# The last six down tiles and the second layer norm in four column chunks, with centred weights and a row sum gathered by DMA

## The chip, the cores and the metric

The kernel runs on one core of a Trainium2 chip. A core has five engines with queues of their own, which work in order: PE (matmuls), DVE (vector), ACT (scalar), POOL (GpSimd) and SP, which here only issues DMAs. POOL issues DMAs too, those that add to their destination among them. The metric is the device time of one execution in microseconds (us), the median of several. The profile is of one execution; it tells times on the chip, a line of the kernel and the names of the tiles for each instruction.

## The reference

One decoder layer runs over 1024 prompt rows and 8 sample rows: three branches with their gates, a layer norm, SwiGLU, a second layer norm. Only the end matters here:

```python
h = layer_norm(ALPHA * x + merged @ w_out, ln1_g, ln1_b)
gt, up = jnp.split(h @ w_gate_up, 2, axis=-1)
h = layer_norm(ALPHA * h + (jax.nn.silu(gt) * up) @ w_down, ln2_g, ln2_b)

def layer_norm(x, g, b):
    xf = x.astype(jnp.float32)
    mu = xf.mean(-1, keepdims=True)
    var = jnp.square(xf - mu).mean(-1, keepdims=True)
    y = (xf - mu) * lax.rsqrt(var + LN_EPS) * g.astype(jnp.float32) + b.astype(jnp.float32)
    return y.astype(x.dtype)
```

The model width is 1024 and the inner width 2816, so `w_down` has 22 blocks of 128 rows. Everything is in 32-bit floats.

## The kernel before

The data lie transposed: the 1024 features of a row are 8 tiles m of 128 partitions, and the 1032 rows (1024 + 8) are columns. A product in full precision is three matmuls, since each operand is split into a rounded high part and the rest: high by high, high by low, low by high (`mm3`, L115). `split` (L77) makes the high part on ACT (L79) and the low part on DVE (L80). Residuals are scaled, so that a product is added with the factor `SHARE`.

`gate_up_down` (L1244) runs the gate and up products and then the first 16 of the 22 blocks of the down product in units, by a scheme with fewer matmuls (7 products in place of 8, `fast_step`). A down unit j ends with two output tiles, zaf and zbf, of the rows m = 2j and 2j + 1; `FinishDown.done` (L1471) has POOL add them by DMA to h, which lies in the chip's memory as `scr_h`. The 16 blocks are done in two rounds of four units each. The last zaf and zbf are those of rows m = 6 and 7.

The last six blocks (`LAST`, blocks 16 to 21) are plain `mm3` products, made in `last_products` (L1344). Their moving operand is g (loaded and split by `last_rows`), their weights are the tiles wl0 to wl7, one for each m, with a raw load in two parts of 512 and 256 columns by SP (`half_raw`, L95, six raw buffers), and a split. `last_weights` is called for the first four from the end of `gate_up_down`, for the others from the first chunk's loop. The 1032 columns are taken in three chunks `CH` of 384, 390 and 258. For each chunk and each m there are 18 matmuls (6 blocks by 3) into a PSUM bank, and one DVE instruction adds the result to a tile acc of the row m, which SP loaded from `scr_h` as a whole (L1342, 516 KB).

The second norm of the chunks 0 and 1 is `layer_norm` (L957), a generator: column sums on DVE, a mean by matmuls with a matrix of ones, subtraction and squares, a variance in the same way, reciprocal root, scaling, affine on ACT, store by SP. It is stepped in the course of the next chunk (at the m in `NORM_AT`). The last chunk has its own, `last_layer_norm` (L992): matmuls with the matrix `shift` (L1019, L1020, L1029, L1030) take a part of the mean out early, sums run on DVE (L1010) and POOL (L1012), and after the last product four full-precision matmuls `le` (L1036 to L1039) give the mean and the mean of squares. Then come the subtraction of the mean in eight tiles on DVE and POOL (L1046), the reciprocal (L1047), eight multiplications (L1050), eight affines on ACT (L1362) and eight stores (L1363).

The order on each engine is decided by a scheduler when the program is built; it follows the order of the code, moved by when inputs are expected. `issue_after` and `behind` tie single instructions to others.

## Time and profile before

| | us |
|---|---|
| median of 3 runs | 1936.51 (1936.05 to 1939.27) |
| the profiled execution | 1938.83 |
| its span in the trace | 1937.1 |
| first product of the last six blocks | 1845.30 |
| last matmul of that stage starts | 1916.32 |
| PE busy | 1901.0 (98%) |
| DVE, ACT, POOL busy | 1389.0, 1001.8, 117.0 |

The page gives busy times, the chain that ended last (each step followed back to what released it), groups of instructions by line, and DMA issues with the time from issue to landing. A row of a timeline has the start, the length, the engine, the line, the operation, output and inputs, and in square brackets how long the engine stood idle before it and what ended that. Where two engines share the words SPq or POOLq, it is the queue of a DMA-issuing engine. Busy shares are means over the whole span: PE's 98% says little on the last 90 us, for which the prediction shows rows.

### The profile page before, as it was taken

The numbers are of one execution on the slowest core, as the hardware profiler recorded it, in microseconds if no ns is written. First come the engines' busy times: TensorE is split into PE (matmuls) and PEld (weight loads), VectorE is DVE, ScalarE is ACT, GpSimd is POOL, SyncE is SP. The second block draws the span as 40 slices with busy tenths as digits, with TensorE's granted clock in tenths as the row PEclk, the third lists the DMA queues.
The fourth block names the chain that finished last, engine by engine and source line by source line (L and its number), as shares of the span: only waits on it lengthen the run. The fifth ranks groups of instructions, "written<-read, shape, count | busy, mean of one in ns | idle before, by whom it ended". The sixth has DMA issues, their size and how long they took to land.

```text
span 1937.1 us, 37999 instructions
## 1 busy us (share of the span) xinstructions
PE 1901.0 (98%) x14716; PEld 1869.5 (97%) x14716; DVE 1389.0 (72%) x2738; ACT 1001.8 (52%) x2115; POOL 117.0 (6%) x168
## 2 busy tenths in 40 slices
PE   9999999999999999999999999999999999999996
PEld 8999999999999998888899999999999999999996
DVE  7878887877866655378887557775667667858467
ACT  6555565555655644388775234543433434636424
POOL 1000001110000000022110000000000000001001
PEclk9999999999999999999999999999999999999998
DMA  8545555446423376667534351123245345768542
GB/s 308 179 146 173 168 182 167 140 150 210 169 83 137 117 240 222 196 173 208 152 98 152 110 197 58 60 99 99 93 154 195 96 134 182 254 161 233 137 143 88
DMA packets 171637, 303.20 MB, mean 157 GB/s; under 512 B 19568, under 2 KB 86208, under 8 KB 171456
## 3 DMA queue, kind: packets, MB, share of 16 engines
q1 hardware_dynamic: 168384, 290.22, 45.8%
q0 software_dynamic: 3072, 10.55, 2.7%
q8 instruction: 115, 1.88, 0.4%
q14 instruction: 66, 0.54, 0.1%
HBM read 214.79 MB, written 90.09 MB: 157 GB/s over the span
## 4 chain that ended last, share of the span: by engine, by line
PE 84%; ACT 5%; DMA 4%; DVE 4%; issue 1%; SPq 0%; ACTq 0%; DVEq 0%
PE ub L250 5%; PE ub L248 5%; PE ub L249 5%; PE ubfg L248 4%; PE ubfg L249 4%; PE ubfg L250 4%; PE ud L250 3%; PE ud L249 3%; PE ud L248 3%; PE udfg L248 2%; PE udfg L249 2%; PE udfg L250 2%; PE op L120 2%; PE op L122 2%; PE op L121 2%; PE brs L120 2%
## 5 line engine op out<-in xcount | busy, mean ns | idle before, releaser
L605 ACT ACTIVATE bp<-bp,bst 128x257 f32<-128x257 f32 (+1 forms) x128 | 62.8, 493 | 17.7 <-DVE bst L601 17.3
L248 PE MATMUL ub<-th,u_4h 128*128 128x258 f32 x240 | 67.8, 283 | 1.3 <-ACT u2s L274 1.3
L248 PE MATMUL ub<-th,u_0h 128*128 128x258 f32 x240 | 68.0, 284 | 0.7 <-ACT zb L1490 0.6
L250 PE MATMUL ub<-th,u_4l 128*128 128x258 f32 x240 | 68.2, 284 | 0.0
L250 PE MATMUL ub<-th,u_0l 128*128 128x258 f32 x240 | 68.2, 284 | 0.0
L250 PE MATMUL ub<-th,u_2l 128*128 128x258 f32 x240 | 68.2, 284 | 0.0
L250 PE MATMUL uc<-th,u_3l 128*128 128x258 f32 x240 | 68.2, 284 | 0.0
L250 PE MATMUL ud<-th,u_1l 128*128 128x258 f32 x240 | 68.1, 284 | 0.0
L250 PE MATMUL ud<-th,u_5l 128*128 128x258 f32 x240 | 68.1, 284 | 0.0
L250 PE MATMUL ub<-th,u_6l 128*128 128x258 f32 x240 | 68.1, 284 | 0.0
L248 PE MATMUL ub<-th,u_6h 128*128 128x258 f32 x240 | 67.9, 283 | 0.0
L248 PE MATMUL uc<-th,u_3h 128*128 128x258 f32 x240 | 67.9, 283 | 0.0
L248 PE MATMUL ub<-th,u_2h 128*128 128x258 f32 x240 | 67.8, 283 | 0.0
L248 PE MATMUL ud<-th,u_5h 128*128 128x258 f32 x240 | 67.8, 282 | 0.0
L248 PE MATMUL ud<-th,u_1h 128*128 128x258 f32 x240 | 67.7, 282 | 0.0
L249 PE MATMUL ub<-tl,u_6h 128*128 128x258 f32 x240 | 67.7, 282 | 0.0
L249 PE MATMUL ud<-tl,u_5h 128*128 128x258 f32 x240 | 67.7, 282 | 0.0
L249 PE MATMUL uc<-tl,u_3h 128*128 128x258 f32 x240 | 67.6, 282 | 0.0
L249 PE MATMUL ub<-tl,u_4h 128*128 128x258 f32 x240 | 67.6, 282 | 0.0
L249 PE MATMUL ud<-tl,u_1h 128*128 128x258 f32 x240 | 67.6, 282 | 0.0
L249 PE MATMUL ub<-tl,u_0h 128*128 128x258 f32 x240 | 67.6, 282 | 0.0
L249 PE MATMUL ub<-tl,u_2h 128*128 128x258 f32 x240 | 67.6, 282 | 0.0
(954 smaller groups left out, 8228.3 us busy)
## 6 DMA issues: line engine op xcount, KB each, us to landing
ur<-win SPq DMA_DIRECT2D x120, 256.0 KB, 2.9
urfg<-wgu SPq DMA_DIRECT2D x80, 256.0 KB, 2.6
scr_f<-G SPq DMA_DIRECT2D x22, 516.0 KB, 3.2
f<-scr_f SPq DMA_DIRECT2D x16, 516.0 KB, 5.7
fs<-scr_t SPq DMA_DIRECT2D x16, 516.0 KB, 8.3
dck<-cmk SPq DMA_DIRECT2D x32, 256.0 KB, 3.7
dcv<-cmvT SPq DMA_DIRECT2D x32, 256.0 KB, 2.8
st<-scr_q SPq DMA_DIRECT2D x32, 256.0 KB, 5.1
```

The source lines that it names most:

```text
L120: nc.tensor.matmul(ps, sh, mh, start=opens and i == 0, stop=False)
L121: nc.tensor.matmul(ps, sh, ml, start=False, stop=False)
L122: self.last_mm = nc.tensor.matmul(ps, sl, mh, start=False, stop=closes and i == last).ins
L248: mm(sh[:, w], xh, start=opens and k == 0, stop=False)
L249: mm(sh[:, w], xl, start=False, stop=False)
L250: self.last_mm = mm(sl[:, w], xh, start=False, stop=k == 3).ins
L605: nc.scalar.activation(x, x, AF.Exp, bias=st[:, g:g + 1], scale=-1.0, accum_out=st[:, 4 + g:5 + g])
```

## The change

The last six blocks and the second norm are done in four chunks q of 258 columns (`QN`). What it rests on: if from each column of `w_down`'s last six blocks' contribution the mean over the 1024 features is taken out of the weights themselves, then the product adds nothing to a row's mean, and the mean is that of h alone, known before the products.

- `weight_means`, stepped in the units of `gate_up_down`, loads the weights of the last six blocks once more (SP, eight loads), sums them on DVE and gives `wbar`, minus the mean for each of the six blocks. `last_weights` adds it, on POOL, to the raw weights before they are split (two instructions for each m, of 512 and 256 columns).
- `row_sums` has POOL gather the sum over m of the rows of h by eight DMAs, the first plain, the others added to the same tile `rsum` in SBUF. It runs in the second round's units 1, 2 and 3. The last zaf and zbf, that are not in h yet when rows 6 and 7 are gathered, are added on DVE (`sums`), which then splits the sum.
- `residual` loads h in blocks r(q, kh) of four rows m and 258 columns (kh = 0: rows 0 to 3, by SP; kh = 1: rows 4 to 7, by POOL, for q = 0 in two halves). `centre` takes the mean from a block, with a mean made by two matmuls on `rsum`.
- `down_norm` does the chunks 0 to 2 (squares, folding, variance, reciprocal root, scaling, affine, a store for each block). The last chunk only squares, adds and has two `le` matmuls; its affines are shared by ACT and DVE.
- The matrix `shift`, `layer_norm` and `last_layer_norm` go.

The core of the diff:

```diff
@@ -1277,6 +1186,10 @@
             self.fast_step(st[u], i, moving[u[0]], finish[u])
             if i == 6:
                 del st[u]
+            if i in (2, 5):
+                next(means, None)
+            if u[0] == FAST - 1 and u[1] and i == 1:
+                self.row_sums(((6, 0, 1), (7, 2, 3), (4, 5))[u[1] - 1])
...
-                        4: lambda: self.last_rows(7, 4), 5: lambda: self.last_weights(0, 0),
-                        6: lambda: self.last_acc(0), 7: lambda: self.last_weights(1, 2),
-                        8: lambda: self.last_acc(1)}.get(n - len(todo) + 10)
+                        4: lambda: self.last_rows(7, 4), 5: self.last_weights,
+                        7: lambda: (self.last_weights(), self.residual(0, 0)),
+                        8: lambda: (self.last_weights(), self.residual(1, 0)), 9: self.last_weights}.get(
+                            n - len(todo) + 10)
...
+    def row_sums(self, rows):
+        for m in rows:
+            if m == 6:
+                self.rsum = self.zt("rsum")
+                self.nc.gpsimd.dma_start(self.rsum, self.scr["h"][:, m, :])
+            else:
+                self.nc.gpsimd.dma_start(self.rsum, self.scr["h"][:, m, :], accum_op=ALU.add)
...
+    def weight_means(self):
+        nc, (f0, nf) = self.nc, LAST
+        part = self.sm.tile([P, KT, nf], F32, tag="wpart", name="wpart", bufs=1)
+        for m in range(KT):
+            raw = self.zt(f"wsum{m}")[:, :nf * P]
+            nc.sync.dma_start(raw, self.io["wdn"][m][:, f0 * P:(f0 + nf) * P])
+            yield
+            nc.vector.tensor_reduce(part[:, m, :], raw.rearrange("p (k n) -> p k n", k=nf), axis=AX.X, op=ALU.add)
+            yield
+        self.wbar = self.sm.tile([P, nf], F32, tag="wbar", name="wbar", bufs=1)
+        nc.vector.tensor_reduce(self.wbar, part.rearrange("p m k -> p k m"), axis=AX.X, op=ALU.add)
+        nc.vector.tensor_scalar_mul(self.wbar, self.wbar, -1.0 / D)
...
+    def last_weights(self):
+        nc, m, (f0, nf) = self.nc, len(self.wl), LAST
+        if m % 2 == 0:
+            self.wslots = self.slot_pairs(m // 2, f"wl{m}")
+        hi, lo = (t.rearrange("p k n -> p (k n)") for t in self.wslots[m % 2])
+        for a, b in ((0, 4), (4, nf)):
+            n, w = (b - a) * P, slice(a * P, b * P)
+            raw = self.half_raw(self.io["wdn"][m][:, (f0 + a) * P:(f0 + b) * P], n, f"wl{m}r{a}")[:, :n]
+            blocks = raw.rearrange("p (k n) -> p k n", k=b - a)
+            nc.gpsimd.tensor_add(blocks, blocks, self.wbar[:, a:b].unsqueeze(2).to_broadcast([P, b - a, P]))
+            self.split(hi[:, w], lo[:, w], raw)
+        self.wl.append([(hi[:, k * P:(k + 1) * P], lo[:, k * P:(k + 1) * P]) for k in range(nf)])
...
+    def residual(self, q, kh):
+        t = self.zt(f"r{q}{kh}").rearrange("p (k n) -> p k n", k=4)
+        src = self.scr["h"][:, 4 * kh:4 * kh + 4, q * QN:(q + 1) * QN]
+        if kh == 0:
+            self.nc.sync.dma_start(t, src)
+        elif q == 0:
+            self.nc.gpsimd.dma_start(t[:, 0:2, :], src[:, 0:2, :])
+            self.nc.gpsimd.dma_start(t[:, 2:4, :], src[:, 2:4, :])
+        else:
+            self.nc.gpsimd.dma_start(t, src)
+        self.A[q, kh] = t
...
+    def sums(self):
+        nc = self.nc
+        mean, spare = self.slot_pairs(4, "rsum")
+        hi, lo = (t.rearrange("p k n -> p (k n)") for t in mean)
+        self.spare = [t.bitcast(F32) for t in spare]
+        for z in self.tail:
+            nc.vector.tensor_add(self.rsum, self.rsum, z)
+        self.split(hi, lo, self.rsum)
+        self.mean = hi, lo
...
+    def centre(self, q):
+        nc = self.nc
+        mu = self.bank("o", f"n2mu{q}")[:, :QN]
+        for n, t in enumerate(self.mean):
+            nc.tensor.matmul(mu, self.ones, t[:, q * QN:(q + 1) * QN], start=n == 0, stop=n == 1)
+        for kh in range(2):
+            nc.vector.tensor_sub(self.A[q, kh], self.A[q, kh], self.spread(mu))
...
+    def down_norm(self, q):
+        nc, r, vec = self.nc, self.A, self.vec
+        yield
+        if q < 2:
+            self.centre(q)
+        sq = self.spare
+        for kh in range(2):
+            nc.scalar.activation(sq[kh], r[q, kh], AF.Square)
+        nc.vector.tensor_add(sq[0], sq[0], sq[1])
+        s = self.fold(sq[0])
+        yield
+        var = self.col_mean(s, QN, f"n2va{q}")
+        rs = self.ph.tile([P, QN], F32, tag="rs", name=f"n2rs{q}", bufs=1)
+        nc.scalar.activation(rs, var, AF.Sqrt, bias=vec[:, V_EPS:V_EPS + 1])
+        nc.vector.reciprocal(rs, rs)
+        for kh in range(2):
+            nc.vector.tensor_mul(r[q, kh], r[q, kh], self.spread(rs))
+            for k in range(4):
+                self.affine(q, kh, k)
+            self.store(q, kh, 0, 4)
...
+        side, s2, sq = [self.down_norm(q) for q in range(3)], row("s2"), None
+        for n in side:
+            next(n)
+        self.sums()
+        for q, kh in ((2, 0), (3, 0), (0, 1), (1, 1), (2, 1), (3, 1)):
+            self.residual(q, kh)
+        go = {(1, 0): (0,), (1, 4): (0,), (2, 0): (1,), (2, 4): (1,), (3, 0): (2,), (3, 3): (2,)}
+        for q in range(4):
             for m in range(KT):
-                ps = product(m)
-                r = rs[m]
-                if m in NORM_AT:
-                    self.norm_step()
+                if len(self.wl) < KT:
+                    self.last_weights()
+                ps = self.bank(("mm", "s")[m % 2], f"dl{m}_{q}")[:, :QN]
+                cols = slice(q * QN, (q + 1) * QN)
+                self.mm3(ps, [(self.wl[m][k], tuple(a[:, cols] for a in self.g[k])) for k in range(nf)])
+                with self.tc.issue_after(self.last_mm):
+                    for n in go.get((q, m), ()):
+                        next(side[n], None)
+                    if (q, m) in ((1, 2), (2, 2)):
+                        self.centre(q + 1)
+                r = self.A[q, m // 4][:, m % 4, :]
                 nc.vector.scalar_tensor_tensor(r, ps, SHARE, r, op0=ALU.mult, op1=ALU.add)
-                if m == 1:
-                    nc.vector.tensor_add(s1, rs[0], r)
-                elif m > 1:
-                    nc.vector.tensor_add(s1, s1, r)
-            self.norm_start(self.layer_norm(c, rs, s1, V_G2, emit, "n2", c == 1))
+                if q == 3:
+                    sq = s2 if m == 0 else ph.tile([P, QN], F32, tag="sq", name=f"lsq{m}", bufs=2)
+                    nc.scalar.activation(sq, r, AF.Square)
+                    if 0 < m < 7:
+                        nc.vector.tensor_add(s2, s2, sq)
+        ones = self.ones.bitcast(F32)
+        e = self.bank("t", "le")[:, :QN]
+        nc.tensor.matmul(e, ones, s2, start=True, stop=False)
+        nc.tensor.matmul(e, ones, sq, start=False, stop=True)
+        rs = row("lrs")
+        nc.scalar.activation(rs, e, AF.Sqrt, bias=self.vec[:, V_EPS:V_EPS + 1])
+        nc.vector.reciprocal(rs, rs)
+        for kh in range(2):
+            nc.vector.tensor_mul(self.A[3, kh], self.A[3, kh], self.spread(rs))
+        for k in range(4):
+            self.affine(3, 0, k)
+            self.store(3, 0, k, k + 1)
+        for k in (3, 2, 1):
+            self.affine(3, 1, k, nc.vector)
+            self.store(3, 1, k, k + 1)
+        self.affine(3, 1, 0)
+        self.store(3, 1, 0, 1, nc.scalar)
```

The first place is POOL, around the last accumulates of zaf and zbf (line L1473 before, L1489 after). Names carry buffer numbers; what stands in brackets are the semaphores that an instruction waits for: DMASW for landings of POOL's DMAs, DMAHW for those of SP's, numbered in turn. Before, POOL's queue at this place is

```order
L1473 DMA scr_h<-zaf_23483 128x1032 [waits DMASW4_49,DVE_49]
L1473 DMA scr_h<-zbf_23516 128x1032 [waits DMASW5_49,Activation_49]
L1473 DMA scr_h<-zaf_23767 128x1032 [waits DMASW6_49,DVE_49]
L1473 DMA scr_h<-zbf_23798 128x1032 [waits DMASW7_49,Activation_49]
L1012 TENSOR_TENSOR ls_24366<-ls_24366,lsq_24510 128x258 [waits DMAHW0_49,DMAHW1_49,PE_49,Activation_49]
```

and now (L1267 is the addition of wbar, L1278 and L1279 are the halves of r(0, 1), L1281 the other r loads of POOL)

```order
L1489 DMA scr_h<-zaf_23796 128x1032 [waits DVE_49]
L1278 DMA r_23961<-scr_h 128x2x258
L1489 DMA scr_h<-zbf_23825 128x1032 [waits Activation_49]
L1267 TENSOR_TENSOR wl4r_23974<-wl4r_23974,wbar 128x512 [waits DMAHW0_49,Pool_49]
L1267 TENSOR_TENSOR wl4r_23979<-wl4r_23979,wbar 128x256 [waits DMAHW1_49,Pool_49]
L1267 TENSOR_TENSOR wl5r_24004<-wl5r_24004,wbar 128x512 [waits DMAHW2_49,Pool_49]
L1279 DMA r_23961<-scr_h 128x2x258 [waits DMASW6_49,DMASW0_49]
L1281 DMA r_23964<-scr_h 128x4x258
L1281 DMA r_23966<-scr_h 128x4x258
L1281 DMA r_23968<-scr_h 128x4x258 [waits DVE_49]
L1267 TENSOR_TENSOR wl5r_24009<-wl5r_24009,wbar 128x256 [waits DMAHW3_49,Pool_49]
L1267 TENSOR_TENSOR wl6r_24038<-wl6r_24038,wbar 128x512 [waits DMAHW4_49,Pool_49]
```

Behind these stand the other additions for wl6 and wl7. The load at L1279 waits for DMASW6 and DMASW0, the landings of the zaf and of the zbf above it; the loads and additions behind it are new on this queue, and the sums `ls` of the last chunk are gone from it.

The second place is PE's end. Before, behind the last products:

```order
L122 MATMUL dl_2_24602<-g7h_23701,wl3l_24062 128x258
L1019 MATMUL dl_2_24602<-c0h_24367,shift 128x258
L1020 MATMUL dl_2_24602<-c0l_24368,shift 128x258
L1036 MATMUL le_24371<-ls_24365,ones 128x258 [waits DVE_49]
L1037 MATMUL le_24372<-ls_24366,ones 128x258 [waits Pool_49]
L1038 MATMUL le_24371<-acc_24102,ones 128x258 [waits DMAHW3_49]
L1039 MATMUL le_24372<-lsq_24624,ones 128x258 [waits Activation_49]
```

Now:

```order
L118 MATMUL dl_3_24758<-g7h_23734,wl6h_24036 128x258
L119 MATMUL dl_3_24758<-g7l_23735,wl6h_24036 128x258
L120 MATMUL dl_3_24758<-g7h_23734,wl6l_24037 128x258
L118 MATMUL dl_3_24758<-g7h_23736,wl6h_24036 128x258
L119 MATMUL dl_3_24758<-g7l_23737,wl6h_24036 128x258
L120 MATMUL dl_3_24758<-g7h_23736,wl6l_24037 128x258
L1382 MATMUL le<-s_23948,ones 128x258 [waits DVE_49]
L1383 MATMUL le<-lsq_24778,ones 128x258 [waits Activation_49]
```

The shift matmuls and two of the four `le` are gone; what PE waits for is the sum of squares from DVE and the last square from ACT.

The third place is DVE, among the first chunk's accumulations (L1374) and the splits of the weights (L78), now:

```order
L1374 SCALAR_TENSOR_TENSOR r_23862<-dl_0_24078,r_23862 128x258 [waits PE_49]
L78 TENSOR_TENSOR wl4l_23973<-wl5r_24009,wl4h_23972 128x256 [waits DMAHW3_49,Activation_49]
L1374 SCALAR_TENSOR_TENSOR r_23961<-dl_0_24098,r_23961 128x258 [waits DMASW7_49,PE_49]
L78 TENSOR_TENSOR wl6l_24035<-wl6r_24038,wl6h_24034 128x512 [waits DMAHW4_49,Activation_49]
L78 TENSOR_TENSOR wl6l_24035<-wl6r_24043,wl6h_24034 128x256 [waits DMAHW5_49,Activation_49]
L78 TENSOR_TENSOR wl6l_24037<-wl7r_24068,wl6h_24036 128x512 [waits DMAHW6_49,Activation_49]
L78 TENSOR_TENSOR wl6l_24037<-wl7r_24073,wl6h_24036 128x256 [waits DMAHW7_49,Activation_49]
L1374 SCALAR_TENSOR_TENSOR r_23961<-dl_0_24118,r_23961 128x258 [waits PE_49]
```

The splits of the weights, whose high part ACT makes from what POOL wrote, stand in the order of the row tiles, and the accumulation of row tile 5 (the last row) stands behind all of them.

157 lines of the change are left out of this document (27 added, 130 removed).

## The prediction

> **What bounds the kernel now.** I read the page's first and fourth parts (shares, chain that ended last), then PE's first and last product of the stage and its few rows behind it, then the stage in windows, then POOL's own timeline, because the change gives POOL work there.
>
> ```profile
> PE 1901.0 (98%) x14716; PEld 1869.5 (97%) x14716; DVE 1389.0 (72%) x2738; ACT 1001.8 (52%) x2115; POOL 117.0 (6%) x168
> ...
> PE 84%; ACT 5%; DMA 4%; DVE 4%; issue 1%; SPq 0%; ACTq 0%; DVEq 0%
> ```
>
> PE is the path; the others come in at the two ends. So a thing counts here only if it alters PE's matmuls, leaves a hole between them, or stands behind the last one. Next, PE by time at the two ends of the stage that is rewritten:
>
> ```profile
> 1845.30 0.34 PE L120 MATMUL dl<-g5h,wl0h 128*128 128x384 f32 x1
> ...
> 1916.32 0.29 PE L1020 MATMUL dl<-c0l,shift 128*128 128x258 f32 x1
> 1919.73 1.23 PE L1036 MATMUL le<-ls,ones 128*128 128x258 f32 x2 [3.12 <-DVE ls L1010]
> 1920.75 1.07 PE L1037 MATMUL le<-ls,ones 128*128 128x258 f32 x2
> 1922.47 1.07 PE L1039 MATMUL le<-lsq,ones 128*128 128x258 f32 x2
> ```
>
> Products run from 1845.30 to 1916.61 (71.31 us). Then comes a tail without products of 20.5 us up to the span's end at 1937.1. The windows say whether the stage has holes (columns: stretch, its length, busy us of PE, PEld, DVE, ACT, POOL with counts, clock, DMA share, GB/s):
>
> ```profile
> 1846.00:1850.00 4.00, 4.00 (x24) 4.00 (x24) 0.00 (x0) 0.24 (x1) 1.55 (x2) 1.00 1.02 341
> 1850.00:1854.00 4.00, 4.00 (x25) 4.00 (x24) 2.94 (x6) 1.09 (x3) 0.00 (x0) 1.00 1.06 281
> 1854.00:1858.00 4.00, 4.00 (x25) 4.00 (x24) 0.00 (x0) 0.00 (x0) 0.00 (x0) 1.00 1.04 263
> 1858.00:1862.00 4.00, 4.00 (x25) 4.00 (x24) 2.30 (x5) 1.86 (x4) 0.00 (x0) 1.00 0.97 371
> ...
> 1899.00:1916.60 17.60, 17.59 (x141) 16.95 (x139) 16.67 (x35) 7.54 (x16) 2.34 (x3) 1.00 0.00 1
> 1916.60:1937.10 20.50, 3.81 (x9) 2.52 (x8) 13.43 (x25) 10.86 (x22) 6.19 (x9) 0.55 0.37 130
> ```
>
> PE is full through the stage at clock 1.00, and the DMA engines are full from 1846 to 1862. That second fact is what the change meets.
>
> **Part 1: the matmuls.** Before, the stage streams 144 matmuls over each of the 1032 columns (8 row tiles, 6 weight blocks, 3 terms), 10 shift matmuls of 258 and 8 column means of 384 or 390 (4 each): 148608 + 2580 + 3096 = 154284 columns in 71.31 us, or 0.462 ns a column, 0.119 us for 258. After, the shifts and those means go; eight matmuls for the four means and six for three variances come, 14 x 258: 152220 columns, 70.36 us. **-0.95 us.** A row tile's 18 matmuls of 258 take 2.15 us, where the first chunk's (384) took 3.2.
>
> **Part 2: the tail.** Its rows now:
>
> ```profile
> 1916.83 0.41 DVE L1021 SCALAR_TENSOR_TENSOR acc<-dl,acc 128x258 f32<-128x258 f32 x1
> 1925.90 1.75 DVE L1047 RECIPROCAL lrs<-lrs 128x258 f32<-128x258 f32 x1
> 1929.09 2.78 DVE L1050 TENSOR_TENSOR acc<-acc,lrs 128x258 f32<-128x258 f32 x8
> ...
> 1918.41 0.42 ACT L1004 ACTIVATE lsq<-acc 128x258 f32<-128x258 f32 x1 [0.46 <-POOL ls L1012]
> 1924.10 0.51 ACT L1044 ACTIVATE lrs<-lrs,vec 128x258 f32<-128x258 f32 x1 [0.22 <-DVE lrs L1043]
> 1928.12 5.63 ACT L1362 ACTIVATE acc<-acc,vec 128x390 f32<-128x390 f32 x11 [3.00 <-DVE acc L979]
> ...
> 1889.28 45.11 SPq L1363 DMA_DIRECT2D o_y<-acc  x24
> ...
> 1840.24 1.82 SPq L1342 DMA_DIRECT2D acc<-scr_h  x4
> ...
> L1077 DVE TENSOR_TENSOR R<-R,n1rs 128x1032 f32<-128x1032 f32 x8 | 9.5, 1228 | 0.1
> ```
>
> Afterwards, from the last product: accumulate 0.41 with the 0.22 before it (0.63); the last addition to s2, about 0.4, beside the last square of 0.42 (1.1); two e pairs of 1.07 (3.2); sqrt 0.51 and a hand-over (3.9); reciprocal 1.75 (5.7); two multiplications of 1.23 over a half block (7.0 and 8.2). Each affine of ACT takes 0.51 (5.63 / 11); its first four end near 9.1, three on DVE at 0.35 (L1050's piece) near 9.3, ACT's fifth near 9.6. Seven stores of SP, about 0.45 apart (an estimate from SP's four loads in 1.82 us), put the last issue's end near 10.5. From the last store's end now (1889.28 + 45.11 = 1934.39) to the span's end are 2.71 us, so the tail is 13.2. Gone are the sums on POOL ahead of the first le (the wait of 3.12), two le pairs, the subtraction of squared means, the eight mean subtractions and the previous chunk's leftovers. **-7.3 us**, with bounds -5.5 (stores at twice the distance) and -8.6 (the second e pair hidden, stores as fast as the affines).
>
> **Part 3: POOL's queue at the start of the stage.** This is the term that decides. What POOL does there now, and how long its two last accumulates into h take to land:
>
> ```profile
> 1845.77 0.88 POOL L1473 DMA_DIRECT2D scr_h<-zaf  x1 [19.06 <-DVE zaf L281]
> 1846.36 1.20 POOL L1473 DMA_DIRECT2D scr_h<-zbf  x1
> ...
> scr_h<-zaf POOLq DMA_DIRECT2D x1, 516.0 KB, 9.4
> scr_h<-zbf POOLq DMA_DIRECT2D x1, 516.0 KB, 12.2
> ...
> scr_h<-zaf POOLq DMA_DIRECT2D x8, 516.0 KB, 5.8
> scr_h<-zbf POOLq DMA_DIRECT2D x8, 516.0 KB, 7.8
> ...
> SPq L1342 <- DMA scr_h<-zaf: 4.1, 1, 4.1
> SPq L1342 <- DMA scr_h<-zbf: 3.0, 1, 3.0
> ```
>
> The two landings, 9.4 and 12.2 us against medians of 5.8 and 7.8, fall into the full DMA window. Today they are waited for by SP, whose queue has only the loads of rows 6 and 7 left; nobody is late. In the changed order POOL issues zaf, half a load of r(0,1), zbf, then adds wbar to wl4 and to four blocks of wl5, and then the second half of r(0,1), which reads rows 6 and 7 and so waits for both landings. Three more r loads stand behind it, and behind those the additions to the rest of wl5, all of wl6 and wl7. An engine's queue is in order, so the weights of row tiles 5 to 7 wait for a transfer that they have nothing to do with.
>
> When are they needed? Row tile 5 starts at 1845.30 + 5 x 2.15 = 1856.1, and the chunk would end at 1862.5. Prices, from POOL's rows and from the splits now:
>
> ```profile
> L401 POOL DMA_DIRECT2D scr_mk<-mkr x8 | 4.6, 570 | 30.8 <-ACT mkr L400 30.8
> L1012 POOL TENSOR_TENSOR ls<-ls,lsq 128x258 f32<-128x258 f32 x6 | 4.9, 816 | 66.9 <-ACT lsq L1004 66.5
> L612 POOL TENSOR_SCALAR bp<-bp,bst 128x256 f32<-128x256 f32 (+1 forms) x32 | 32.2, 1006 | 128.1 <-DVE bst L606 126.8 <-ACT bph L79 1.3
> 1859.04 0.93 ACT L79 CAST wl3h<-wl6r 128x512 fp32r<-128x512 f32 x2 [7.68 <-DMA wl6r<-wdn]
> 1859.70 1.03 DVE L80 TENSOR_TENSOR wl3l<-wl6r,wl3h 128x512 fp32r<-128x512 f32 x2 [6.52 <-ACT wl3h L79]
> ```
>
> - zbf's issue slips by the half load to about 1847.4. Its landing: 7.8 us (median) to 12.2 (this place) later. SP's competing traffic shrinks from eight acc loads to four r loads, so I take 10, between: 1857.4.
> - The four r loads: no row shows a load with 1032-byte pieces issued by POOL. 128 pieces of 1 KB cost 0.57 (L401), 128 rows of 4 KB 0.88. If the price is by instruction, 4 x 0.57 = 2.3; if by piece, (2 + 4 + 4 + 4) x 0.57 = 8.0. I take 5.4, between, and POOL is free at 1862.8.
> - Five additions: three of 256 columns at 0.8 (L1012, 258), two of 512 at 1.5 (twice, less a fixed part): 5.4 us. Upper bound by L612's 1.0 for 256: 7.0.
> - The split of four blocks takes 1.3 (0.6 + 0.7), and row tile 7 then needs 2.15. The last 512-addition ends 0.8 us before the last 256: 5.4 - 0.8 + 1.3 + 2.15 = 8.1, so the chunk ends at 1870.9, not 1862.5. **+8.4 us**, bounds 3.1 (landing 7.8, issues 2.3) and 14.8 (landing 12.2, issues 8.0, additions 7.0).
>
> A page of the Trainium skill would have this term vanish: "DMA: Bandwidth & Descriptors", "Anatomy of one DMA — SWDGE (gpsimd) path", fits the time of such a DMA as about 2.0 us plus its bytes over 436e3, which for 516 KB would be an estimate of 3.2 us. The rows here do not agree: 9.4 and 12.2.
>
> **Part 4: the rest.** The weight sums (8 loads, 8 reductions of 128x768 on DVE) fall in the gate units, under PE, and the row sums' eight POOL DMAs in the last three down units, where a row of PE and POOL reads
>
> ```profile
> 1800.00:1820.00 20.00, 20.00 (x169) 20.00 (x168) 9.61 (x18) 7.04 (x15) 1.76 (x2) 1.00 0.46 93
> ...
> 1822.62 0.86 POOL L1473 DMA_DIRECT2D scr_h<-zaf  x1 [16.09 <-DVE zaf L281]
> ```
>
> PE has no hole, the DMA engines are half free, and POOL waits 16 to 19 us between a zbf and the next zaf. Two or three landings of 5.8 us a unit fit there, and I cost them at nothing; if that cover fails, a late zaf adds its own delay to part 3. From chunk 1 on DVE has per chunk 8 accumulates (3.3), four mean subtractions (4.9), sum and folds (2.3), a split (0.4), the reciprocal (1.75) and two multiplications (2.5): 15.1 of 17.2 us, less than the 16.67 of 17.60 which it bears now.
>
> **Sum.** -0.95 - 7.3 + 8.4 = +0.15 us. The profiled execution took 1938.83 us with a span of 1937.1, 2.3 above the median of 1936.51; the difference is applied to the median: 1936.7, given as 1937.
>
> **Rivals.**
> - *The tail's gain stays, the queue hardly stalls.* Landings at their medians and issues priced by instruction: stall 3.1, sum -5.1, 1931.4. For it: half of the competing loads are gone, the r loads are spread. Against: the window is full, and zbf has the longest landing of its eight. By the page's 3.2 us the stall would be under 1 us and the time about 1929; that is the far end of this rival, with 0.05 of its chance.
> - *Slower: the weights behind the landing cost more than the tail gives.* One mechanism, at the second half of r(0,1): from a stall of 12.2 us on (sum above +3.9) it decides. At 12.2 for the landing and 8.0 for the issues it is 13.2 to 14.8, sum +5.0 to +6.6, 1941.5 to 1943. For it: the landing is the one measured there, and small pieces may be priced one by one. Against: a megabyte less of acc on the same engines.
> - *The tail is not cut*: chunk 2's norm is late on DVE (two multiplications of 1.23 among the last four accumulates), so the last square waits. Up to 2.5 us back, sum +2.6, 1939. It stays inside the forecast's band.
> - *The change does not do what it says*: its mean chain (eight accumulating DMAs in a row) lands after the first chunk and holds PE at the first centring. With 6 us a landing it is ready before 1846, so I give it little; price some 5 us, 1942.
>
> **How the numbers follow.** A measurement of this kernel tells a change of over 0.2% (3.9 us) from none. Forecast with the third rival (1932.6 to 1940.4): 0.53. First rival: 0.22, all faster. Second: 0.21; the fourth: 0.04, both slower. Range 1930 to 1945: the low ends of parts 2 and 3 together (-0.95 - 8.6 + 3.1 = -6.5) and their high ends (-0.95 - 5.5 + 14.8 = +8.3), without the page's end.
>
> **What would show it.** A wait of PE in chunk 0, near row tiles 5 to 7, for ACT or DVE splits of wl5 to wl7, which wait for POOL at the line that adds wbar, itself behind a wait for scr_h<-zbf; its length is the stall. Products ending near 1924 instead of 1916.6; a tail near 13 us with no sums on POOL; PE without holes from the second chunk on. The forecast is wrong if zbf lands within 8 us, if an r load's issue is below 0.6 or above 2 us, or if PE waits for a mean.

## The result and the profile after

| | before | changed |
|---|---|---|
| median of 4 runs each, us | 1936.28 (1935.49 to 1939.27) | 1949.11 (1947.93 to 1951.31) |
| profiled execution, us | 1938.83 | 1947.93 |
| its span, us | 1937.1 | 1945.9 |

The ratio is 1.0068 [1.0055, 1.0081]: 0.68% slower, and outside the range. The profiled executions lie 2.5 above and 1.2 below their medians, so the traces explain 8.8 us of span where the medians differ by 12.8.

The page after, shares of busy time and the chain that ended last:

```profile
PE 1901.8 (98%) x14852; PEld 1871.6 (96%) x14852; DVE 1390.3 (71%) x2708; ACT 999.9 (51%) x2108; POOL 134.5 (7%) x186
...
PE 85%; ACT 4%; DVE 4%; DMA 4%; issue 2%; SPq 0%; POOL 0%; POOLq 0%; DVEq 0%; ACTq 0%
```

PE has as much busy time as before in a longer span, so nearly all of the loss is idle time. What PE waited for from 1700 us on (us in total, times, longest):

```profile
PE dl L118 <- ACT wl4h L77: 13.0, 1, 13.0
PE ubf L244 <- ACT u2sf L270: 1.8, 1, 1.8
```

These are the two longest; one wait of 13.0 us in the first chunk is most of the story. The split weights are named by pairs of row tiles: wl4 stands for the row tiles 4 and 5, wl6 for 6 and 7. PE's timeline at its two sides, and where the chunk begins and the next begins:

```profile
1844.03 0.28 PE L118 MATMUL dl<-g5h,wl0h 128*128 128x258 f32 x1
...
1856.17 0.28 PE L120 MATMUL dl<-g6h,wl4l 128*128 128x258 f32 x1
...
1869.47 0.58 PE L118 MATMUL dl<-g7h,wl4h 128*128 128x258 f32 x1 [13.02 <-ACT wl4h L77]
...
1871.87 0.58 PE L120 MATMUL dl<-g7h,wl4l 128*128 128x258 f32 x1 [1.61 <-DVE wl4l L78]
...
1877.84 0.37 PE L120 MATMUL dl<-g5h,wl6l 128*128 128x258 f32 x1
1878.05 0.29 PE L118 MATMUL dl<-g6h,wl6h 128*128 128x258 f32 x1
1878.17 0.28 PE L119 MATMUL dl<-g6l,wl6h 128*128 128x258 f32 x1
...
1879.48 0.28 PE L118 MATMUL dl<-g5h,wl0h 128*128 128x258 f32 x1
```

By 1856.3 PE has done 102 matmuls: row tiles 0 to 4 (90) and the first four blocks of row tile 5 (12). The last two blocks need the 256-column part of wl5. After the hole the starts lie 0.21 apart until 1878.05, and 0.12 from then on. Windows show the clock behind it (stretch, length, busy us of PE, PEld, DVE, ACT, POOL with counts, granted clock, DMA share, GB/s):

```profile
1844.00:1856.00 12.00, 12.00 (x102) 12.00 (x101) 7.67 (x13) 3.04 (x5) 5.31 (x6) 1.00 1.07 302
1856.00:1870.00 14.00, 0.98 (x6) 0.74 (x4) 0.56 (x1) 0.40 (x1) 4.73 (x7) 0.68 0.46 132
...
1874.00:1878.00 4.00, 4.00 (x20) 4.00 (x20) 0.87 (x3) 0.00 (x0) 0.00 (x0) 0.50 0.00 0
1878.00:1882.00 4.00, 4.00 (x36) 4.00 (x35) 0.59 (x2) 0.00 (x0) 0.00 (x0) 1.00 0.00 0
```

PE runs behind the hole at a granted clock of 0.50 and does 20 matmuls in 4 us where it otherwise does 36. The Trainium skill, "TensorE: Matmul & The Clock Gate", section "Part 1: The HAM clock gate", says that the clock is halved after an idle window of about 3.4 us and comes back after about as long of sustained work; the trace agrees in kind, but here the low clock lasts some 8.5 us after the restart, with the second wait of 1.61 in it; the last section says from these traces when it falls and when it comes back.

POOL's timeline says why wl5's rest came so late:

```profile
1846.40 1.25 POOL L1489 DMA_DIRECT2D scr_h<-zbf  x1
...
1852.41 1.04 POOL L1267 TENSOR_TENSOR wl5r<-wl5r,wbar 128x512 f32<-128x512 f32 x1 [1.10 <-DMA wl5r<-wdn]
1857.43 0.77 POOL L1279 DMA_DIRECT2D r<-scr_h  x1 [3.99 <-DMA scr_h<-zbf]
1858.19 0.81 POOL L1281 DMA_DIRECT2D r<-scr_h  x1
1863.09 0.77 POOL L1281 DMA_DIRECT2D r<-scr_h  x1 [4.09 <-issue]
1867.59 0.75 POOL L1281 DMA_DIRECT2D r<-scr_h  x1 [3.74 <-issue]
1868.35 0.62 POOL L1267 TENSOR_TENSOR wl5r<-wl5r,wbar 128x256 f32<-128x256 f32 x1
1868.93 1.61 POOL L1267 TENSOR_TENSOR wl6r<-wl6r,wbar 128x512 f32<-128x512 f32 x2
1870.50 1.79 POOL L1267 TENSOR_TENSOR wl7r<-wl7r,wbar 128x512 f32<-128x512 f32 x2
```

POOL waits for zbf's landing until 1857.43, then issues four r loads until 1868.35, before two of which it stands still for 4.09 and 3.74 us, and only then adds wbar to wl5's rest. "issue" means that it waited for nothing that the profile shows.

The tail, on PE and DVE:

```profile
1932.85 0.28 PE L120 MATMUL dl<-g7h,wl6l 128*128 128x258 f32 x1
1934.31 0.70 PE L1382 MATMUL le<-s,ones 128*128 128x258 f32 x2 [1.18 <-DVE s L1379]
...
1937.80 2.38 DVE L1388 TENSOR_TENSOR r<-r,lrs 128x1032 f32<-128x1032 f32 x2
```

From the last product's end (1933.13) to the span's end are 12.8 us, where there were 20.5.

By stages, from PE's starts: the first product of the down units (both rounds, eight units) starts at 1680.38 (before: 1683.17). Up to there the changed kernel has only the weight sums more, and the gate units, in which they run, take 404.6 us from their first product to this point, where they took 404.5. The kernels below that have the same code up to there reach that point between 1678.7 and 1683.4, so this is scatter of single executions. From there to the first product of the last six blocks: 163.6 (162.1). The last six blocks: 89.1 (71.3). Tail: 12.8 (20.5). So 8.8 = -2.8 + 1.5 + 17.8 - 7.7.

### The profile page after: what moved, and what is told of

It is laid out like the page before. It is cut to its first block, busy times and chain, and to the rows that moved or that the text cites. A ratio compares the mean times of both kernels' runs of the same rounds, so it can differ in the third digit from the quotient of the medians.

```text
span 1945.9 us, 38254 instructions
## 1 busy us (share of the span) xinstructions
PE 1901.8 (98%) x14852; PEld 1871.6 (96%) x14852; DVE 1390.3 (71%) x2708; ACT 999.9 (51%) x2108; POOL 134.5 (7%) x186
## 4 chain that ended last, share of the span: by engine, by line
PE 85%; ACT 4%; DVE 4%; DMA 4%; issue 2%; SPq 0%; POOL 0%; POOLq 0%; DVEq 0%; ACTq 0%
PE ub L244 5%; PE ub L246 5%; PE ub L245 5%; PE ubfg L245 4%; PE ubfg L246 4%; PE ubfg L244 4%; PE ud L246 3%; PE ud L244 3%; PE ud L245 2%; PE udfg L244 2%; PE udfg L245 2%; PE udfg L246 2%; PE op L118 2%; PE op L120 2%; PE op L119 2%
## 5 line engine op out<-in xcount | busy, mean ns | idle before, releaser
L601 ACT ACTIVATE bp<-bp,bst 128x257 f32<-128x257 f32 (+1 forms) x128 | 62.8, 493 | 17.7 <-DVE bst L597 10.6
```

The source lines that it names most:

```text
L601: nc.scalar.activation(x, x, AF.Exp, bias=st[:, g:g + 1], scale=-1.0, accum_out=st[:, 4 + g:5 + g])
```

## The experiments

Each ratio is to the kernel before, measured together with it; its own median was 1935.5 to 1937.2 in these measurements, so compare rows by their ratios. "Down units" is the stretch from the first product of the down units (both rounds) to the first of the last six blocks, "last blocks" the stretch from there to the last product's end, both from PE's starts in each profile. The mark * stands where rows are left out of the row sum.

| | median, us | ratio to before | down units | last blocks |
|---|---|---|---|---|
| before | 1936.28 | 1 | 162.1 | 71.3 |
| changed | 1949.11 | 1.0068 [1.0055, 1.0081] | 163.6 | 89.1 |
| r_on_sp | 1935.33 | 0.9995 [0.9985, 1.0004] | 168.3 | 72.0 |
| r_pool_last | 1933.49 | 0.9981 [0.9972, 0.9991] | 167.8 | 71.0 |
| r_between | 1937.88 | 1.0008 [0.9999, 1.0017] | 167.5 | 75.0 |
| fill_hole | 1949.87 | 1.0066 [1.0051, 1.0081] | 163.8 | 89.4 |
| adds_on_dve | 1938.31 | 1.0009 [0.9996, 1.0021] | 169.3 | 73.8 |
| r_halves | 1937.01 | 0.9996 [0.9983, 1.0009] | 165.1 | 78.1 |
| early_sums | 1937.30 | 0.9998 [0.9985, 1.0011] | 170.2 | 71.0 |
| changed_early_sums | 1949.73 | 1.0063 [1.0048, 1.0078] | 166.4 | 86.9 |
| dve_early | 1933.96 | 0.9995 [0.9984, 1.0005] | 168.6 | 71.0 |
| no_rows_4_5 * | 1931.38 | 0.9968 [0.9957, 0.9979] | 165.9 | 71.0 |
| no_row_sums * | 1927.73 | 0.9959 [0.9943, 0.9974] | 162.3 | 71.3 |
| sums_in_gate | 1937.70 | 1.0008 [0.9999, 1.0018] | 161.8 | 72.0 |
| sums_mid_gate | 1938.70 | 1.0012 [1.0002, 1.0021] | 162.2 | 72.1 |

### Is it POOL's queue?

**r_on_sp**: the four late r loads go to SP, behind the last weight load.

```diff
-            self.nc.gpsimd.dma_start(t[:, 2:4, :], src[:, 2:4, :])
+            self.behind(self.nc.sync.dma_start(t[:, 2:4, :], src[:, 2:4, :]).ins, self.last_load)
         else:
-            self.nc.gpsimd.dma_start(t, src)
+            self.behind(self.nc.sync.dma_start(t, src).ins, self.last_load)
...
-        for q, kh in ((2, 0), (3, 0), (0, 1), (1, 1), (2, 1), (3, 1)):
+        for q, kh in ((2, 0), (3, 0)):
+            self.residual(q, kh)
+        while len(self.wl) < KT:
+            self.last_weights()
+        for q, kh in ((0, 1), (1, 1), (2, 1), (3, 1)):
```

> The second half of r(0,1) and r(1,1), r(2,1), r(3,1) are loaded by SP behind its last weight load instead of by POOL; all weight additions are built before them; nothing else changes. Theory 1 (the order of POOL's queue makes the hole, and the slow clock behind the hole is its consequence): PE waits under 2 us in the first chunk, the clock stays at 1.00, about 18.7 us less than the changed kernel (13.3 + 1.9 of holes, some 3.7 of matmuls at half clock), so 1930 to 1932. Theory 2 (the weights of row tiles 5 to 7 are late by themselves: raw loads, POOL additions and splits in a row): a hole of 8 us or more stays, 1943 or more.

**r_pool_last**: the same, but the loads stay on POOL, behind the last addition of wbar (`self.last_add`).

> The same loads stay on POOL, but stand behind all weight additions in its queue. Theory 1: no hole at row tiles 5 to 7, 1930 to 1934; the gaps of about 4 us between the r loads stay on POOL and now hide, with at most a short DVE wait for r(2,1). Theory 2: 1943 or more, as with SP.

**r_between**: only the new order of the code, without `behind`; one half load then stands ahead of wl5's rest, one load ahead of wl7.

> All last_weights are built before the r loads, so that POOL's order has only the second half of r(0,1) ahead of wl5's rest and one r load ahead of wl7. POOL then still waits 4 us for the landing of zbf, but no addition waits behind a second 512-piece load. Theory 1: the hole is what the landing alone makes, 3 to 5 us of PE waits in the first chunk, 1935 to 1938. Theory 2: 1943 or more. If the landing alone made most of the hole (a third theory, the serial r loads would only hide behind it): a hole of 10 us or more, 1943 or more.

In the first two the hole is gone: the last blocks take 72.0 and 71.0. But r_on_sp is no faster than the kernel before and misses its 1930 to 1932. POOL in r_pool_last:

```profile
1860.19 1.79 POOL L1267 TENSOR_TENSOR wl7r<-wl7r,wbar 128x512 f32<-128x512 f32 x2 [0.36 <-DMA wl7r<-wdn]
1861.93 0.77 POOL L1279 DMA_DIRECT2D r<-scr_h  x1
1862.69 0.81 POOL L1281 DMA_DIRECT2D r<-scr_h  x1
1868.00 0.76 POOL L1281 DMA_DIRECT2D r<-scr_h  x1 [4.50 <-issue]
1872.45 0.75 POOL L1281 DMA_DIRECT2D r<-scr_h  x1 [3.69 <-issue]
```

The gaps in the r loads are as long as in the changed kernel, but nothing waits behind them. From the changed kernel to r_pool_last are 15.6 us by the medians (16.8 by the ratios); the order on one queue cost that. In the profiles the last blocks give back 18.1, of which the down units take 4.2. r_pool_last, 0.19% faster than before, beats both kernels. In r_between the half load still waits 5.24 us for zbf, with idle times of PE of 3.0 us in all. But the gain stops short of the tail's 7.7 us, and the down units have grown by 5 to 6 us. PE's longest wait there in r_pool_last:

```profile
PE ubf L244 <- ACT u2sf L270: 3.4, 1, 3.4
```

This second loss is taken up below.

**adds_on_dve**: the changed kernel, with the additions on DVE; the r loads keep their place.

```diff
-            nc.gpsimd.tensor_add(blocks, blocks, self.wbar[:, a:b].unsqueeze(2).to_broadcast([P, b - a, P]))
+            nc.vector.tensor_add(blocks, blocks, self.wbar[:, a:b].unsqueeze(2).to_broadcast([P, b - a, P]))
```

> The changed kernel with one word changed: wbar is added to the weights by DVE instead of POOL. POOL's queue keeps all its loads in the same order, with the wait for zbf and the gaps between the r loads, but no addition stands behind them. Theory 1: the hole of 13 us at row tile 5 goes although the loads are as late as before; DVE takes 9 us more work beside PE, so up to 3 us of small waits in the first chunk; 1930 to 1934. If the lateness of the r blocks themselves held PE (through DVE's accumulations): a hole of 8 us or more stays, 1943 or more.

POOL's late r loads come about as late as before: 11.4 to 22.5 us behind the first product (1852.66), where the changed kernel has 13.4 to 23.6. POOL's timeline, and PE's two longest waits:

```profile
1864.01 0.75 POOL L1279 DMA_DIRECT2D r<-scr_h  x1 [9.48 <-DMA scr_h<-zbf]
...
1875.16 0.75 POOL L1281 DMA_DIRECT2D r<-scr_h  x1 [4.01 <-issue]
```

```profile
PE ubf L244 <- ACT u2sf L270: 5.0, 1, 5.0
PE dl L120 <- DVE wl4l L78: 1.6, 1, 1.6
```

So the late r data themselves hold nobody: what they carried with them was the additions behind them in the queue. The last blocks fall from 89.1 to 73.8. The time misses its 1930 to 1934, since the wait in the down units is the longer one now: DVE stood still for 4.3 and 2.6 us ahead of additions to wl0 and wl1, whose loads had not landed, and the first g load was issued 2.2 us later in the down units than in the changed kernel.

**fill_hole**: the changed kernel with 96 idle matmuls ahead of row tile 5, to keep PE at work in the hole.

```diff
+                if (q, m) == (0, 5):
+                    dum = self.bank("t", "dum")[:, :QN]
+                    for i in range(96):
+                        self.last_mm = nc.tensor.matmul(dum, self.wl[4][0][0], self.g[0][0][:, :QN], start=i == 0, stop=i == 95).ins
```

> The changed kernel with 96 extra matmuls of 258 columns into an unread bank between row tiles 4 and 5, some 11.5 us of PE work inside the hole of 13 us. If the half clock behind the hole comes from PE's idleness: the clock stays at 1.00 behind it and the time falls by 3 to 4 us, 1945 to 1946. If it has another cause, or the hole only shifts: 1949 to 1950.

The time did not fall. The extra matmuls ran from 1858.6 to 1870.1, and the clock was still 1.00 behind them. wl5's rest came 2.5 us later in this execution, PE waited 1.90 us for its split, and then 16 matmuls ran at half clock:

```profile
1872.58:1875.99 3.41, 1.57 (x11) 1.37 (x12) 3.41 (x5) 1.92 (x4) 2.21 (x3) 1.00 0.25 103
1875.99:1879.41 3.42, 3.42 (x19) 3.42 (x18) 1.39 (x4) 0.00 (x0) 0.00 (x0) 0.50 0.00 0
```

So the half clock does come from PE's idleness, but a wait of 1.9 us was enough for it. The run doesn't settle what the low clock by itself costs.

### What holds the r loads back?

**r_halves**: r_pool_last, each whole r load of POOL (512 pieces of 1032 bytes) as two of 256.

```diff
-            self.behind(self.nc.gpsimd.dma_start(t, src).ins, self.last_add)
+            for i in (0, 2):
+                self.behind(self.nc.gpsimd.dma_start(t[:, i:i + 2, :], src[:, i:i + 2, :]).ins, self.last_add)
```

> r_pool_last with r(1,1), r(2,1), r(3,1) in two loads of 256 pieces each. Theory P (POOL holds a load back while too many pieces of earlier ones are still out, with the bound between 768 and 1024): the first three halves go out back to back and each later one waits about 1 to 3 us, so the last is issued some 5 to 7 us after the first; the time is that of r_pool_last. Theory Q (each POOL load with several pieces a partition waits until the one before has landed): every half waits about 3 us, 15 us or more from first to last.

POOL after the additions:

```profile
1866.11 0.77 POOL L1279 DMA_DIRECT2D r<-scr_h  x1
1866.87 1.49 POOL L1282 DMA_DIRECT2D r<-scr_h  x2
1869.67 1.45 POOL L1282 DMA_DIRECT2D r<-scr_h  x2 [1.32 <-issue]
1873.21 1.44 POOL L1282 DMA_DIRECT2D r<-scr_h  x2 [2.09 <-issue]
```

Three loads (768 pieces) go out without a gap, then POOL waits 1.32 and 2.09 us instead of 4.50 and 3.69; from the first issue to the last one's start it takes 7.8 us, with whole loads 10.5. An issue costs 0.75 whether it has 256 or 512 pieces. Each load that is held back is issued some 0.3 us behind the landing of an earlier one. In the changed kernel the load of 1858.19 takes 4.6 us to land, to 1862.8, and the next is issued at 1863.09; that one takes 4.2, to 1867.3, and the next follows at 1867.59. In r_halves the load of 1866.11 takes 3.2, to 1869.3, and the held one is issued at 1869.67. That fits a limit on the pieces that are issued and not landed, between 768 and 1024 (theory P, whose 5 to 7 us were a little short), and not a price by piece or by instruction, nor theory Q's 15 us. No row shows the limit itself. The kernel's time doesn't bear on this: in it wl4 landed late (its first addition started at 1855.83), which left waits of 3.4 us and a stretch at half clock.

### What costs 5 to 6 us in the down units?

What comes late there is g: its tiles come from the chip's memory, ACT casts them, and u2sf stands behind those casts. ACT in the changed kernel:

```profile
1833.86 1.05 ACT L77 CAST g7h<-g7l 128x1032 fp32r<-128x1032 f32 x1 [2.65 <-DMA g7l<-scr_f]
1834.81 0.65 ACT L270 ACTIVATE u2sf<-ubf 128x258 f32<-128x258 f32 x2
```

The same stretches in windows, before and then changed:

```profile
1820.00:1832.00 12.00, 12.00 (x102) 12.00 (x101) 4.08 (x7) 3.98 (x9) 1.72 (x2) 1.00 0.70 147
1832.00:1845.00 13.00, 12.71 (x105) 12.47 (x104) 11.01 (x19) 9.31 (x18) 0.00 (x0) 1.00 0.78 280
```

```profile
1820.00:1832.00 12.00, 12.00 (x102) 12.00 (x101) 4.12 (x7) 5.34 (x11) 4.06 (x4) 1.00 0.93 211
1832.00:1845.00 13.00, 11.18 (x93) 10.97 (x93) 9.65 (x18) 7.38 (x14) 4.92 (x4) 1.00 1.01 302
```

The DMA engines were 0.70 to 0.78 busy and are full now; PE loses 1.5 us.

**no_rows_4_5**: r_pool_last without the DMAs that add rows 4 and 5, which are then missing from the mean. **no_row_sums**: r_pool_last with row 6 alone in the row sum; no row is added by DMA any more.

```diff
-                self.row_sums(((6, 0, 1), (7, 2, 3), (4, 5))[u[1] - 1])
+                self.row_sums(((6, 0, 1), (7, 2, 3), ())[u[1] - 1])
...
+                self.row_sums(((6,), (), ())[u[1] - 1])
```

> On r_pool_last: the two row-sum DMAs of rows 4 and 5 are left out, so the mean lacks these rows and the output is not the reference's; everything else is unchanged. Theory C: PE's wait at ubf falls below 0.7 us and the time to 1927 to 1930. Rival: the wait stays, 1932 or more.

> r_pool_last without seven of the eight row-sum DMAs (only row 6 is loaded), so the mean is not the reference's. What all row sums cost together: by theory C', which counts the collisions of the whole chain, PE's wait at ubf is below 1 us and no slow matmuls follow, 1926 to 1929. If the additions on POOL, which slow DVE and so zaf, make the g loads late: the wait stays at 2 us or more, 1930 or more.

Without the row sums the down units are back at 162.3, and the wait is:

```profile
PE ubf L244 <- ACT u2sf L270: 0.5, 1, 0.5
```

The row sums cost r_pool_last 5.8 us by the medians (4.3 by the ratios; no_row_sums has three runs). Rows 4 and 5 are a part only: without them the wait is still 2.5, and the time lies between the two that were expected. Windows around the wait in r_pool_last, and then in no_row_sums:

```profile
1836.00:1840.00 4.00, 2.69 (x12) 2.69 (x13) 2.63 (x3) 3.98 (x7) 1.30 (x2) 0.54 1.04 332
1840.00:1844.00 4.00, 4.00 (x24) 4.00 (x23) 4.00 (x9) 2.13 (x5) 2.70 (x3) 0.61 0.96 237
```

```profile
1836.00:1840.00 4.00, 4.00 (x36) 4.00 (x35) 4.00 (x9) 1.63 (x5) 2.56 (x2) 1.00 1.01 333
```

In r_pool_last too a wait of a few us is followed by some 25 matmuls at half speed (2.4 us).

That the row sums cost this is shown; the way is not. The DMA share is as high without them (1.01 above), so full DMA engines alone do not make the wait. Nor must a row sum be under way beside g: in no_rows_4_5 the last one had landed 1.8 us before the first g load was issued, and this load took 9.1 us (5.6 before). The traces show a second way. The additions to wl0 and wl1 stand behind row sums on POOL and come late, and in r_pool_last a DVE instruction beside them took 2.95 us in place of 0.69. zaf, behind it on DVE, was issued 140.8 us after the first down product, and not 139.5 as in the changed kernel. In the four kernels whose zaf came at 139.9 to 141.0 with g issued on time (r_pool_last, r_on_sp, r_between, no_rows_4_5), the first g load took 8.4 to 9.2 us; where zaf came at 139.5 to 139.7, 5.1 to 6.7, with the row sums or without. No run takes the two ways apart, and kernels with the same row sums wait from 1.7 us (r_halves) to 4.2 (r_on_sp).

**early_sums**, **changed_early_sums**, **dve_early**: r_pool_last, the changed kernel and adds_on_dve, each with the row sums one unit earlier and the zaf and zbf of unit 2 added on DVE in the last unit.

```diff
-            if u[0] == FAST - 1 and u[1] and i == 1:
-                self.row_sums(((6, 0, 1), (7, 2, 3), (4, 5))[u[1] - 1])
+            if u[0] == FAST - 1 and i == 1:
+                if u[1] < 3:
+                    self.row_sums(((6, 7, 4), (5, 0, 1), (2, 3))[u[1]])
+                else:
+                    for z in self.tail:
+                        nc.vector.tensor_add(self.rsum, self.rsum, z)
```

> On r_pool_last: the row sums are gathered one unit earlier (rows 6, 7, 4 in unit 0, 5, 0, 1 in unit 1, 2, 3 in unit 2), and the zaf and zbf of units 2 and 3 are added on DVE, so that no row sum is gathered while SP loads g6 and g7. Theory C (the row sums of rows 4 and 5 on the full DMA engines make the g loads late, ACT's cast of g7 holds u2sf behind it, PE waits 2 to 4 us at ubf and runs at half clock for a while): the wait at ubf falls below 0.7 us, no half clock before the products, 4 to 6 us less than r_pool_last, 1927.5 to 1929.5, the fastest of all. Rival (the g loads are late from the other loads, the weights' or zaf and zbf): the wait stays at 3 us or more, 1932 to 1934.

> The changed kernel with the row sums gathered earlier in the same way, and its r loads on POOL left where they are. Theory C with theory 1: the wait at ubf goes (2 to 4 us with the slow matmuls behind it), the hole of 13 us at row tile 5 stays: 1944.5 to 1947. Rival: no change, 1949. If the hole itself came from the row sums: below 1938.

> adds_on_dve with the row sums gathered one unit earlier as in early_sums. Theory D (in early_sums the chain of row sums held the additions for wl0 and wl1 on POOL, these the raw buffers, these SP's load of wl2 and the g loads behind it): with the additions on DVE nothing waits behind the chain, SP issues the g loads no later than the kernel before does, PE's wait at ubf falls below 1.5 us; 1926 to 1930, the fastest. Rival (the collision on the DMA engines alone makes the g loads late, whoever adds): the wait at ubf stays at 2.5 us or more and the time at 1930 to 1935.

The wait on u2sf stays: 5.8 in early_sums, 3.1 in changed_early_sums and 4.1 in dve_early. But the edit brings a wait of its own. The addition of zaf to rsum stands in DVE's queue and waits for the last row sum to land, in early_sums:

```profile
1828.69 1.23 DVE L1196 TENSOR_TENSOR rsum<-rsum,zaf 128x1032 f32<-128x1032 f32 x1 [7.28 <-DMA rsum<-scr_h]
```

In dve_early it waits 3.04 us, in changed_early_sums 2.07. Behind it on DVE stands the split uf_3l, SP's load for wl2 waits for that split, and the g loads stand behind wl2 on SP: the first is issued 149.2, 147.6 and 146.4 us after the first down product (early_sums, dve_early, changed_early_sums), and at 142.8 in r_pool_last and before. So these three runs don't tell what row sums at an earlier place cost, and theories C and D are not decided by them.

**sums_in_gate**, **sums_mid_gate**: r_pool_last with the row sums out of the down rounds, one row in each of eight gate units, from number 6 on in the first and from number 11 on in the second. The later one copies wbar into rsum first, so that it can't start ahead of the weight means. All zaf and zbf of both rounds are then added on DVE, and rsum has a buffer of its own, for which the pool z gives up one of ten.

```diff
+            if u[0] == "g" and i == 1 and 11 <= u[1] < 11 + KT:
+                self.row_sum(u[1] - 11)
...
+            self.nc.vector.tensor_copy(self.rsum[:, :LAST[1]], self.wbar)
...
-            self.zbufs = 10
+            self.zbufs = 9
...
-        self.b.tail = za, zb
+        for z in (za, zb):
+            self.b.nc.vector.tensor_add(self.b.rsum, self.b.rsum, z)
```

> r_pool_last with the eight row-sum DMAs moved into the gate units, where h has only the first norm's output, and every zaf and zbf of the down units added to the sum on DVE (16 additions of 1.2 us in units where DVE is half idle); rsum has a buffer of its own, the other blocks share nine instead of ten. Nothing is left out. Theory C' (all the row sums' traffic in the last down units makes zaf, zbf and the g loads collide): PE's wait at ubf is below 1 us with no slow matmuls, as without row sums, 1926 to 1930, faster than both kernels. If DVE's additions delay zaf or the splits instead, or nine buffers hold the gate units up: 1931 or more, with waits of PE in the gate or down units.

> sums_in_gate with the chain of row sums held until the weight means are done (about 1428 us, by a copy of wbar into rsum ahead of the first gather), so that it runs beside the middle gate units, whose DMA engines are half idle, and no longer beside the first norm's stores and the first gate loads at 1250 to 1300. Nothing is left out. Theory C' with the first gate units' 10 us as what sums_in_gate lost: no wait of PE at ubfg, ubf from about 1681, PE's wait at ubf below 1 us without slow matmuls, 1926 to 1929, faster than both kernels. If the nine buffers or DVE's 16 additions cost it: the gate or down units stay longer, 1933 or more.

Both free the down units (161.8 and 162.2, no wait on u2sf), which agrees with no_row_sums. But their gate units take 414.6 and 415.7 us, where r_pool_last has 404.6, so both miss their forecasts and are no faster than before. PE's waits in the gate units of sums_mid_gate, and a window around the chain's end:

```profile
PE ubfg L246 <- DVE ufg_0l L78: 3.4, 1, 3.4
PE ubfg L244 <- ACT zbfg L1466: 3.2, 2, 2.8
```

```profile
1480.00:1520.00 40.00, 37.23 (x298) 37.02 (x298) 24.69 (x36) 14.41 (x30) 0.87 (x1) 0.96 0.58 177
```

The first wait is that of the first gate unit, long before the chain (1433 to 1484), where the weight loads meet a pool with nine buffers; the second is beside the chain. So more than the chain costs there. Ahead of the chain nothing of the edit acts but the lost buffer; no run has that loss alone. A place for the row sums that costs nothing was not found.

## Why the prediction was wrong, point by point

- **Part 1, matmuls (-0.95).** Small and mostly not seen: without holes the last blocks take 71.0 (r_pool_last), 0.3 less than before, where 70.36 was worked out.
- **Part 2, tail (-7.3).** Right: 12.8 us against 13.2 forecast, by the steps named: one wait for the sum of squares (1.18), two multiplications (2.38), affines on both engines. That it is so close is in part luck: the multiplications start 4.7 us behind the last product, not 5.7, and what follows takes 8.1, not 7.5.
- **Part 3, POOL's queue (+8.4, bounds 3.1 to 14.8).** The place and the mechanism are right, the size is wrong; it came to 18.3: the first chunk ends at 1879.48 and not, from 1844.03 with 144 products of 0.119, at about 1861.2. zbf's landing was met (1857.4), with luck: it was issued 1.0 earlier than assumed and took 10.6, not 10. **The failed term is the four r loads**: 5.4 us assumed, 8.0 at most; they took 10.9 (1857.43 to 1868.35), 7.8 of it two gaps, waits for the landing of the load before, that the prices by instruction and by piece both missed. It was said that the forecast is wrong if a load's issue comes above 2 us; it came to 2.7 a load. From POOL free to the chunk's end 8.1 us were counted, and 11.1 passed: the additions were shorter (3.9 for 5.4), but PE had 40 matmuls left at 1871.87, not one row tile of 18, and did 28 of them at the low clock (the 40 took 7.6 us and not 4.8). The low clock after a hole was in no term. The stage also began 1.3 us earlier while the landing stayed where it was. The three, 5.5, 3.0 and 1.3, make up the 9.9 that were missing.
- **Part 4, the rest (0).** The weight sums did cost nothing (404.6 for 404.5 us of gate units). The row sums did not: down units longer by 1.5 us in the changed kernel's profile, and 4.3 to 5.8 us in r_pool_last. The row that was read (1800 to 1820, DMA share 0.46) is not where they meet g: from 1820 on the share was 0.70 to 0.78 before the change. Cover was looked for under PE and in POOL's idle time, and not for the loads of g and the additions on POOL, which the row sums make late.
- **The rivals.** "Slower, at the second half of r(0,1)" is the one that came, 6 to 8 us beyond its price of 1941.5 to 1943. Its point of decision, a stall above 12.2, held. The tail was cut, and the mean chain holds nobody at the first centring: the two mean matmuls start at 1881.6, between products without a wait. By the estimate from the Trainium skill, "DMA: Bandwidth & Descriptors", "Anatomy of one DMA — SWDGE (gpsimd) path", a landing takes 3.2 us; the trace does not agree, zbf took 10.6.

What the runs show: the order of POOL's queue cost 15.6 us (changed to r_pool_last), which contains the landing, the loads' gaps and the low clock; the row sums cost 4 to 6 us more in r_pool_last; the tail gives back 7.7. How much of the 15.6 is the low clock alone was not isolated; in the changed kernel's profile it is about 3 us of the last blocks (30 matmuls, each some 0.1 longer).

## What to carry to other kernels

On an engine that works in order and issues DMAs too, put every load that nobody needs soon behind the work that others wait for, and price its issue by the gaps between such loads and not by the length of the instruction. Before a DMA is costed at nothing because engines are idle, read the very stretches in which it will run, and ask whose loads, and whose work behind it in a queue, it will delay. A hole in PE can cost more than its length, since PE may start again at a lower clock. And when an experiment moves work, look whether the moved work waits for something itself: the additions of early_sums did, and held DVE.

## What the runs showed of the hardware

- POOL holds back a load of 512 pieces while another of that size is out, and issues it some 0.3 us behind its landing: gaps of 3.6 to 4.9 us in every kernel that has three such loads in a row, shown as "issue" (one of them, in dve_early, as a wait for DVE); with loads of 256 pieces the gaps are 1.3 and 2.1.
- From the first down product to the last product, PE's granted clock fell to 0.50 in 13 stretches of these fifteen traces, each 3.41, 6.83 or 17.07 us long, so one, two or five times 3.41. Windows of that length, laid from the changes of the clock, separate them. Each began at the end of 3.41 us in which PE was idle for 1.72 us or more (1.72 in r_halves, 1.84 in fill_hole); up to 1.60 us in such a piece brought none. Each ended behind the first 3.41 us without idle time; with 0.68 us idle (changed kernel, 1871.2 to 1874.6) the clock stayed low. So the length of one wait does not decide it: 1.72 us in r_halves lay in one piece and cost 16 slow matmuls, 1.82 at the same place in the changed kernel lay across two and cost none.
- Accumulating DMAs of 516 KB land late where the DMA engines are full, and a second one right behind the first later still: zaf of the last unit but one took 5.4 to 6.6 us over these kernels and zbf behind it 7.4 to 10.1; the last pair took 8.0 and 10.6 in the changed kernel.
